# Last layer of a two-layer diffusion trunk: residual and experts' sums on rows of tokens instead of columns

## Chip, cores, metric

One core of one Trainium2 chip. The metric is the device time of one execution in microseconds; lower is better.

## What is computed

A trunk of two layers over 512 latent and 256 context tokens of 1024 channels, batch 1. Each layer adds a token mixer (convolution and RWKV-7 scans) and a hierarchical mixture of 32 experts to the residual, each with a gate per channel (g1, g2). In the last layer only the latent tokens go on. A last RMSNorm with a weight per channel closes the trunk. What the change touches:

```python
# last layer, h2 = modulated norm of x
y2 = hier_moe(h2)            # each token: top group, top 2 experts of 32
                             # sum over both of  gate[token, j] * w2(silu(w1 h2) * (w3 h2))
x = x + g2 * y2              # g2: one number per channel
return x * rsqrt(mean(x*x, axis=-1) + 1e-6) * final_g
```

All data are fp32.

## The kernel before

The residual `xm` is held by columns: channels on the 128 partitions (8 groups, KT = 8), tokens along the free dimension; the latent tokens are its columns from 256 on (`NC_`). In the last layer the 256 columns before them are free.

`moe` (L1154) runs the last stage of a layer. `route` makes, on DVE, for each expert a list of up to 64 tokens (`slot`), the place of its results in the DRAM buffer `bufY` (`dst`), and the gate of each token (`gates`). Then come 32 times `block`: POOL gathers the expert's 64 rows of tokens from DRAM (`xe`), PE turns them to columns, DVE adds the shift (`xs`), PE multiplies with w1 and w3 (streamed, 1 MB a piece, six pieces an expert), ACT and DVE add the halves (`hs`), PE turns again, ACT and DVE make `hid`, PE multiplies with w2 into `py`, ACT and DVE add its halves into `yo` (L1438, L1439), 64 rows of 1024 channels, and POOL scatters these rows into `bufY` (L1440). `route_rest` is called after the first `block` and makes what only the end needs: `rows`, the places in `bufY` of each token's two results, and the sums for the gates. The pieces of w1, w2 and w3 go through three rings of buffers (`er` 5, `ez` 9, `ex` 3); SP issues a load when PE has freed the buffer, in a fixed rotation, so at most 17 pieces lie ahead. `overflow` is a loop over experts with more than 64 tokens; in the profiled execution its body runs no time in the last layer, but all engines pass through its start and its end.

`combine` follows. For each of four tiles of 128 tokens POOL gathers the two rows of every token (`cy`, eight gathers of 512 KB). DVE makes two diagonal matrices from the tokens' gates (`dg`, L1486), PE multiplies with them, which weights the rows, adds the two and turns them to columns (L1493), and DVE adds the result times g2 to `xm` (L1496, 8 per tile). ACT squares (L1499), PE sums the squares over channels with a column of ones (L1501), DVE makes the inverse root for a pair of tiles (`rs_cols`, L295 to L303), PE spreads it over the partitions (`spread`, L309), and DVE writes `xm * final_g * r` (L1510, 8 per pair of tiles). SP stores the pair: two transfers of 1 MB.

The order of the instructions on an engine is fixed when the program is built. Outside of regions marked as ordered by hand a planner picks, with estimated times, the instruction that comes first in the program among those that are ready; it is not bound to the program's order. The `overflow` loop is a border that no instruction crosses. In `route` DVE, ACT and POOL are ordered by hand among themselves.

[...] SBUF buffers named `hs` are two, shared with another tag.

Of the kernel before, what the change touches and what calls it, by code (L numbers as in the profile page):

```python
# [9 lines left out]
F32 = mybir.dt.float32  # L10
# [3 lines left out]
AF = mybir.ActivationFunctionType  # L14
ALU = mybir.AluOpType
# [3 lines left out]
P = 128  # L19
D = 1024  # L20
KT = 8
NC_ = 256
NL = 512
T = NC_ + NL
# [22 lines left out]
CAP = 64  # L47
# [68 lines left out]
class Trunk:  # L116
# [1037 lines left out]
    def moe(self):  # L1154
        nc, tc, t, l, k = self.nc, self.tc, self.t, self.l, self.k
        self.route()
        self.pp.release()
        self.pp = tc.alloc_tile_pool(name=f"pM{l}", bufs=1, space=PSUM)
        self.bp = tc.alloc_tile_pool(name=f"bp{l}", bufs=1, side=self.B, reuse_waits="tile")
        self.gathered = []  # L1160
        with tc.manual_schedule(engines={mybir.EngineType.Pool}):
            for e in range(2):
                self.gathered.append(self.gather(self.slot[:, e:e + 1], True))
        self.prefetch(RING[l][2])
        for e in range(NE):
            self.block(self.slot[:, e:e + 1], lambda: self.dst[:, e:e + 1],
                       t["w1"][l, e], t["w3"][l, e], t["w2"][l, e])
            if e == 0:
                self.route_rest()
        n = 1 if self.full else 0  # L1170
        for i in range(n):
            e = nc.values_load(self.ovt[0:1, i:i + 1], engines=[mybir.EngineType.SP], min_val=0, max_val=NE - 1)
            self.block(self.slot_over[:, i:i + 1], lambda: self.dst[:, NE + i:NE + i + 1], *self.chosen(e))
        self.overflow(n)
        self.bp.release()
        self.ep2.release()
        self.ep.release()
        self.combine()
        self.pp.release()
        self.mp.release()  # L1180

    def route(self):
        e = mybir.EngineType
        with self.tc.manual_schedule(engines={e.DVE, e.Activation, e.Pool}):
            self.route_ordered()
        self.rp.release()
# [213 lines left out]
    def block(self, slot, dst, w1, w3, w2):  # L1400

        nc, k = self.nc, self.k
        xe = self.gathered.pop(0) if self.gathered else self.gather(slot)
        ps = self.psum("px", [P, KT, CAP], 2)
        for kt in range(KT):
            nc.tensor.transpose(ps[:, kt, :], xe[:, kt * P:(kt + 1) * P], k["ident"][:CAP, :CAP])  # L1408
        xs = self.sb(self.wp, [P, 512], "xs", bufs=3, tag="wr")[:].rearrange("p (k t) -> p k t", k=KT)
        nc.vector.tensor_tensor(xs, ps, self.mod[:, 24:32, 0:1].to_broadcast([P, KT, CAP]), op=ALU.add)  # L1410

        def mm(out, a, src, nk, n):
            step = 2048 // n
            for g in range(0, nk, step):
                w = self.ahead.pop(0) if self.ahead else self.expert_weights(src, g, n)
                for i in range(0, step, 2):
                    for c in range(0, n, 512):
                        for h in range(2):
                            kt = g + i + h
                            nc.tensor.matmul(out[h * CAP:(h + 1) * CAP, c:c + 512], a[:, kt, :],  # L1420
                                             w[:, i + h, c:c + 512], start=kt < 2, stop=kt >= nk - 2)

        pt = self.psum("pt", [P, 2, 4, CAP])
        for i, w in enumerate((w1, w3)):
            ps = self.psum("pd", bufs=3)
            mm(ps, xs, w, KT, 512)
            hs = self.hs()[:CAP, :]
            nc.scalar.activation(hs, ps[CAP:], AF.Copy)  # L1428
            nc.vector.tensor_tensor(hs, ps[:CAP], hs, op=ALU.add)  # L1429
            for c in range(4):  # L1430
                nc.tensor.transpose(pt[:, i, c, :], hs[:, c * P:(c + 1) * P], k["ident"][:CAP, :CAP])
        hid = self.sb(self.bp, [P, 4, CAP], "hid", bufs=2)
        nc.scalar.activation(hid, pt[:, 0], AF.Silu)  # L1433
        nc.vector.tensor_tensor(hid, hid, pt[:, 1], op=ALU.mult)  # L1434
        py = self.psum("py", [P, D])
        mm(py, hid, w2, 4, D)
        yo = self.sb(self.bp, [P, D], "yo", bufs=3)[:CAP, :]
        nc.scalar.activation(yo, py[CAP:], AF.Copy)  # L1438
        nc.vector.tensor_tensor(yo, py[:CAP], yo, op=ALU.add)  # L1439
        nc.gpsimd.indirect_dma_start(out=self.bufY[:], out_offset=bass.IndirectOffsetOnAxis(ap=dst(), axis=0), in_=yo,  # L1440
                                     in_offset=None, bounds_check=(NE + NOV) * CAP - 1, oob_is_err=False)

# [4 lines left out]
    def overflow(self, n0):  # L1447
# [3 lines left out]
        with tc.For_i(n0, n, 1) as i:  # L1451
# [4 lines left out]
            nc.sync.dma_start(dst, self.dst[:, bass.ds(NE + i, 1)])  # L1456
            self.block(slot[:], lambda: dst[:], *self.chosen(e))

    def combine(self):

        nc, tc, t, l, k = self.nc, self.tc, self.t, self.l, self.k
        V = nc.vector
        x, lo = self.xm, self.t0
        if not self.last:
            self.normed(self.B)
            self.x_dram = self.dram.tile([P, KT, T], F32, name="x1")
        with tc.tile_pool(name="co", bufs=1, side=self.B, reuse_waits="tile") as cp:
            fg = self.sb(cp, [P, KT], "fg")
            nc.sync.dma_start(fg, t["fg"])
            W = 2 * P  # L1470
            for i0 in (2, 4, 0)[:self.nt // 2] if self.full else (0, 2):
                tok = slice(lo + i0 * P, lo + i0 * P + W)
                s = self.seg(i0)
                sq = self.sb(cp, [P, KT, W], "sq")
# [1 line left out]
                for i in (i0, i0 + 1):  # L1476
                    y = []
                    for j in range(2):
                        g = self.sb(cp, [P, D], f"cy{j}", bufs=4)
                        nc.gpsimd.indirect_dma_start(  # L1480
                            out=g[:], out_offset=None, in_=self.bufY[:],
                            in_offset=bass.IndirectOffsetOnAxis(ap=self.rows[:, i, j:j + 1], axis=0))
# [5 lines left out]
                    for g in range(2):  # L1488
                        ps = self.psum("pd", [P, 4, P], bufs=3)
                        for c in range(4):  # L1490
                            q = slice((4 * g + c) * P, (4 * g + c + 1) * P)
                            for j in range(2):
                                nc.tensor.matmul(ps[:, c, :], y[j][:, q], dg[:, j, :], start=j == 0, stop=j == 1)  # L1493
                        for c in range(4):
                            q = 4 * g + c
# [4 lines left out]
                    for q in range(KT):  # L1500
                        nc.tensor.matmul(pn[:, i - i0:i - i0 + 1], sq[:, q, u], k["ones"][:, :1],  # L1501
                                         start=q == 0, stop=q == KT - 1)
                r = self.rs_cols(cp, pn, 2, 1.0 / D, 1e-6, "c")
                ps = self.psum("px", [P, W], 2)
                for i in range(2):
                    self.spread(ps[:, i * P:(i + 1) * P], r[:, i])
                o = self.sb(cp, [P, KT, W], "fo", bufs=2)
                if self.last:
                    for q in range(KT):
                        V.scalar_tensor_tensor(o[:, q, :], x[:, q, tok], fg[:, q:q + 1], ps, op0=ALU.mult, op1=ALU.mult)  # L1510
                    nc.sync.dma_start(t["out"][:, :, i0 * P:i0 * P + W], o)
                    continue
                nc.sync.dma_start(self.x_dram[:, :, tok], x[:, :, tok])
                n = self.L[l + 1]
                for q in range(KT):
                    b = n["mod"][:, q, s:s + 1]
# [3 lines left out]
                                           op0=ALU.add, op1=ALU.subtract)  # L1520
# [59 lines left out]
```

## Time and profile before

| | us |
|---|---|
| median of three runs | 2935.67 (2931.19 to 2941.17) |
| profiled execution | 2936.51 |
| its span, first to last instruction | 2934.7 |
| experts of the last layer, first transposes to last sum | 2368.7 to 2886.65 |
| first gather of `combine` to the end | 2891.4 to 2934.7 |

Over the span PE is busy 83%, DVE 44%, ACT 29%, POOL 14%; the DMA engines move 251 GB/s on average. These shares are means over stages of different kinds and say little about the last 570 us, in which the change lies. [...]

### The profile page before, as it was taken

To read this page: it belongs to the slowest core of one execution; us is meant where nothing else is said; L and a number is where in the kernel's file an instruction comes from. 1 tells how busy PE (TensorE), PEld (TensorE's weight loads), DVE (VectorE), ACT (ScalarE), POOL (GpSimd) and SP (SyncE) were. 2 spreads that over 40 slices of the span, in tenths; PEclk is the share of its full clock that TensorE was granted. 3 is DMA by queue.
4 is the path that set the end of the run, shared out by engine and by line. 5 is a ranking of instruction groups with operands and counts; after the bars stand their busy time and mean duration, and the time that the engine had idled before them with its cause. 6 is when DMAs were issued, how large, how long until landed. Compare 5 with 4: busy or idle time off the path is not lost. (4 is left out here: it accounts for less than half of the span.)

```text
span 2934.7 us, 43704 instructions
## 1 busy us (share of the span) xinstructions
PE 2445.0 (83%) x17177; PEld 1557.8 (53%) x17177; DVE 1304.1 (44%) x2757; ACT 852.2 (29%) x1637; POOL 403.5 (14%) x509
## 2 busy tenths in 40 slices
PE   6898899998889496778877998788988769697886
PEld 4676677777778232223326775566766633232334
DVE  4576654636463321112225685566546422122223
ACT  4444333333223121111112553343432401111111
POOL 0122011111100101101102231011210011111101
PEclk9899998999999698888997998789989879897898
DMA  7657554553563999999965367454445599999983
GB/s 292 211 153 226 168 169 159 185 172 111 173 216 112 329 403 401 385 397 395 404 256 180 112 192 241 162 171 163 152 130 183 213 350 403 404 401 404 405 354 113
DMA packets 287136, 737.13 MB, mean 251 GB/s; under 512 B 57168, under 2 KB 144464, under 8 KB 230864
## 3 DMA queue, kind: packets, MB, share of 16 engines
q1 hardware_dynamic: 272208, 697.59, 65.7%
q0 software_dynamic: 13280, 31.48, 3.3%
q10 hardware_dynamic: 1440, 5.24, 0.4%
q8 instruction: 136, 2.23, 0.3%
q14 instruction: 72, 0.59, 0.1%
HBM read 647.44 MB, written 99.88 MB: 255 GB/s over the span
## 5 line engine op out<-in xcount | busy, mean ns | idle before, releaser
L332 PE MATMUL pd<-hh,wh 128*128 128x512 f32 (+1 forms) x912 | 354.2, 428 | 16.5 <-ACT wh L313 7.9
L332 PE MATMUL pd<-hh,wl 128*128 128x512 f32 (+1 forms) x912 | 312.5, 383 | 10.1 <-DVE wl L314 10.1
L332 PE MATMUL pd<-hl,wh 128*128 128x512 f32 (+1 forms) x912 | 311.6, 382 | 1.1 <-DVE hl L314 1.1
L1420 PE MATMUL pd<-ez,xs 128*64 128x512 f32 x1072 | 266.7, 608 | 12.4 <-DMA ez<-in_w 12.4
L314 DVE TENSOR_TENSOR wl<-wr,wh 128x512 fp32r<-128x512 f32 x236 | 166.5, 706 | 241.3 <-ACT wh L313 240.7
L1420 PE MATMUL pd<-er,xs 128*64 128x512 f32 x640 | 183.2, 669 | 75.4 <-DMA er<-in_w 75.4
L1428 ACT ACTIVATE hs<-pd 64x512 f32<-64x512 f32 x130 | 75.4, 592 | 574.0 <-PE pd L1420 500.8
L313 ACT ACTIVATE wh<-wr 128x512 fp32r<-128x512 f32 x236 | 148.5, 630 | 286.5 <-PE pd L332 169.3
L1429 DVE TENSOR_TENSOR hs<-pd,hs 64x512 f32<-64x512 f32 x130 | 87.2, 680 | 300.7 <-ACT hs L1428 300.7
L332 PEld LDWEIGHTS pd<-hh,wh 128*128 128x128 f32 x912 | 163.9, 198 | 100.0 <-issue 34.6
L332 PEld LDWEIGHTS pd<-hh,wl 128*128 128x128 f32 x912 | 163.9, 198 | 46.2 <-DVE wl L314 13.5
L332 PEld LDWEIGHTS pd<-hl,wh 128*128 128x128 f32 x912 | 165.3, 199 | 29.4 <-DVE hl L314 2.1
L1420 PE MATMUL py<-ez,hid 128*64 128x512 f32 x560 | 154.1, 688 | 24.9 <-DVE yo L1439 24.9
L1420 PEld LDWEIGHTS pd<-ez,xs 128*64 128x64 f32 x1072 | 83.1, 141 | 155.7 <-issue 129.3
L1410 DVE TENSOR_TENSOR xs<-px,mod 128x512 f32<-128x512 f32 x65 | 44.9, 690 | 240.3 <-PE pd L1420 153.8
L1395 POOL DMA_INDIRECT xe<-h2rows,slot x64 | 61.1, 954 | 624.1 <-PE px L1408 569.5
L1420 PEld LDWEIGHTS pd<-er,xs 128*64 128x64 f32 x640 | 51.5, 152 | 174.1 <-issue 90.5
L1434 DVE TENSOR_TENSOR hid<-hid,pt 128x256 f32<-128x256 f32 x65 | 27.0, 415 | 215.4 <-ACT hid L1433 215.4
L1420 PE MATMUL pd<-ex,xs 128*64 128x512 f32 x368 | 103.5, 654 | 22.1 <-DMA ex<-in_w 22.1
L1439 DVE TENSOR_TENSOR yo<-py,yo 64x1024 f32<-64x1024 f32 x65 | 78.9, 1214 | 94.4 <-ACT yo L1438 82.6
L1440 POOL DMA_INDIRECT bufY<-yo,dst x65 | 59.7, 918 | 349.3 <-DVE yo L1439 218.5
L1420 PEld LDWEIGHTS py<-ez,hid 128*64 128x64 f32 x560 | 47.6, 158 | 112.7 <-issue 104.0
(379 smaller groups left out, 4447.0 us busy)
## 6 DMA issues: line engine op xcount, KB each, us to landing
ez<-in_w SPq DMA_DIRECT2D x204, 1024.0 KB, 16.2
er<-in_w SPq DMA_DIRECT2D x120, 1024.0 KB, 16.4
ex<-in_w SPq DMA_DIRECT2D x66, 1024.0 KB, 17.3
wm<-in_w_mod SPq DMA_DIRECT2D x48, 1024.0 KB, 6.6
wr<-in_w_in SPq DMA_DIRECT2D x172, 256.0 KB, 3.2
bufY<-zrow SPq DMA_DIRECT2D x28, 512.0 KB, 6.7
dKB<-KB SPq DMA_DIRECT2D x16, 768.0 KB, 5.1
dRR<-RR SPq DMA_DIRECT2D x16, 768.0 KB, 4.7
```

What stands on the lines that cost most here:

```text
L313: self.nc.scalar.activation(hi, src, AF.Copy)
L314: self.nc.vector.tensor_tensor(lo, src, hi, op=ALU.subtract)
L332: nc.tensor.matmul(p, a[:, k], h[:, kt, s], start=kt == 0 and j == 0, stop=kt == nk - 1 and j == 2)
L1395: self.nc.gpsimd.indirect_dma_start(out=xe[:], out_offset=None, in_=self.h2[:], in_offset=bass.IndirectOffsetOnAxis(ap=slot, axis=0), boun ...
L1410: nc.vector.tensor_tensor(xs, ps, self.mod[:, 24:32, 0:1].to_broadcast([P, KT, CAP]), op=ALU.add)
L1420: nc.tensor.matmul(out[h * CAP:(h + 1) * CAP, c:c + 512], a[:, kt, :], w[:, i + h, c:c + 512], start=kt < 2, stop=kt >= nk - 2)
L1428: nc.scalar.activation(hs, ps[CAP:], AF.Copy)
L1429: nc.vector.tensor_tensor(hs, ps[:CAP], hs, op=ALU.add)
L1434: nc.vector.tensor_tensor(hid, hid, pt[:, 1], op=ALU.mult)
L1439: nc.vector.tensor_tensor(yo, py[:CAP], yo, op=ALU.add)
L1440: nc.gpsimd.indirect_dma_start(out=self.bufY[:], out_offset=bass.IndirectOffsetOnAxis(ap=dst(), axis=0), in_=yo, in_offset=None, bounds_ch ...
```

## The change

In the last layer alone:

- `row_consts`, before the first expert: loads final_g and makes g2 and final_g into rows that stand on all partitions (`grow`, `frow`), kept in the free columns of `xm`. Each takes 8 DVE products with the identity, 8 PE products with a matrix of ones, 2 ACT copies.
- `turn(kt)`, before experts 1 to 8: PE turns the four 128x128 squares of one channel group of `xm` to rows of tokens, ACT copies them back in place.
- In each `block`: `yo` is multiplied by `grow` on DVE ahead of the scatter (also in the body of `overflow`).
- `combine_rows` instead of `combine`: eight gathers into eight buffers of their own; for each tile two scalar_tensor_tensor on 128x1024 (a row times the token's gate, plus the residual; the other row times its gate, plus that); a square with a sum along the row on ACT; the inverse root per pair; one scalar_tensor_tensor (times r, times `frow`); a store of 512 KB per tile. PE is not used.
- The output tensor has rows of tokens instead of columns.

Layer 0 keeps `combine`; its branches for the last layer are cut out.

```diff
--- before.py
+++ after.py
@@ -1162,7 +1162,11 @@
             for e in range(2):
                 self.gathered.append(self.gather(self.slot[:, e:e + 1], True))
         self.prefetch(RING[l][2])
+        if self.last:
+            self.row_consts()
         for e in range(NE):
+            if self.last and 1 <= e <= KT:
+                self.turn(e - 1)
             self.block(self.slot[:, e:e + 1], lambda: self.dst[:, e:e + 1],
                        t["w1"][l, e], t["w3"][l, e], t["w2"][l, e])
             if e == 0:
@@ -1175,9 +1179,41 @@
         self.bp.release()
         self.ep2.release()
         self.ep.release()
-        self.combine()
+        if self.last:
+            self.combine_rows()
+        else:
+            self.combine()
         self.pp.release()
         self.mp.release()
+
+    def row_of(self, n, col):
+
+
+        nc, k = self.nc, self.k
+        row = self.xm[:, 4 * n:4 * n + 4, :NC_]
+        for g in range(2):
+            ds = self.hs()[:].rearrange("p (a b) -> p a b", a=4)
+            ps = self.psum("pd", [P, 4, P], 3)
+            for c in range(4):
+                nc.vector.tensor_scalar(ds[:, c, :], k["ident"], col[:, 4 * g + c:4 * g + c + 1], None, op0=ALU.mult)
+                nc.tensor.matmul(ps[:, c, :], k["ones"], ds[:, c, :], start=True, stop=True)
+            nc.scalar.activation(row[:, 2 * g:2 * g + 2], ps[:].rearrange("p (a c) b -> p a (c b)", a=2), AF.Copy)
+        return row
+
+    def row_consts(self):
+
+        fg = self.sb(self.mp, [P, KT], "fg")
+        self.nc.sync.dma_start(fg, self.t["fg"])
+        self.grow = self.row_of(0, self.mod[:, 40:48, 0])
+        self.frow = self.row_of(1, fg)
+
+    def turn(self, kt):
+
+        nc = self.nc
+        ps = self.psum("pd", [P, 4, P], 3)
+        for i in range(4):
+            nc.tensor.transpose(ps[:, i, :], self.xm[:, kt, NC_ + i * P:NC_ + i * P + P], self.k["ident"])
+        nc.scalar.activation(self.xm[:, kt, NC_:], ps[:].rearrange("p a b -> p (a b)"), AF.Copy)
 
     def route(self):
         e = mybir.EngineType
@@ -1437,6 +1473,9 @@
         yo = self.sb(self.bp, [P, D], "yo", bufs=3)[:CAP, :]
         nc.scalar.activation(yo, py[CAP:], AF.Copy)
         nc.vector.tensor_tensor(yo, py[:CAP], yo, op=ALU.add)
+        if self.last:
+            yg = yo.rearrange("p (a b) -> p a b", a=4)
+            nc.vector.tensor_tensor(yg, yg, self.grow[:CAP], op=ALU.mult)
         nc.gpsimd.indirect_dma_start(out=self.bufY[:], out_offset=bass.IndirectOffsetOnAxis(ap=dst(), axis=0), in_=yo,
                                      in_offset=None, bounds_check=(NE + NOV) * CAP - 1, oob_is_err=False)
 
@@ -1456,19 +1495,45 @@
             nc.sync.dma_start(dst, self.dst[:, bass.ds(NE + i, 1)])
             self.block(slot[:], lambda: dst[:], *self.chosen(e))
 
+    def combine_rows(self):
+
+        nc, tc, t = self.nc, self.tc, self.t
+        V = nc.vector
+        with tc.tile_pool(name="co", bufs=1, side=self.B, reuse_waits="tile") as cp:
+            ys = []
+            for i in range(4):
+                for j in range(2):
+                    y = self.sb(cp, [P, D], f"cy{i}{j}")
+                    nc.gpsimd.indirect_dma_start(
+                        out=y[:], out_offset=None, in_=self.bufY[:],
+                        in_offset=bass.IndirectOffsetOnAxis(ap=self.rows[:, i, j:j + 1], axis=0))
+                    ys.append(y)
+            for i0 in (0, 2):
+                ss = self.sb(cp, [P, 2], "ss", bufs=2)
+                for i in (i0, i0 + 1):
+                    a, b = ys[2 * i], ys[2 * i + 1]
+                    av = a[:].rearrange("p (k c) -> p k c", k=KT)
+                    V.scalar_tensor_tensor(av, av, self.gates[:, i, 0:1], self.xm[:, :, NC_ + i * P:NC_ + i * P + P],
+                                           op0=ALU.mult, op1=ALU.add)
+                    V.scalar_tensor_tensor(b, b, self.gates[:, i, 1:2], a, op0=ALU.mult, op1=ALU.add)
+                    nc.scalar.activation(a, b, AF.Square, accum_out=ss[:, i - i0:i - i0 + 1])
+                r = self.rs_cols(cp, ss, 2, 1.0 / D, 1e-6, f"c{i0}")
+                for i in (i0, i0 + 1):
+                    b = ys[2 * i + 1]
+                    bv = b[:].rearrange("p (a c) -> p a c", a=4)
+                    V.scalar_tensor_tensor(bv, bv, r[:, i - i0], self.frow, op0=ALU.mult, op1=ALU.mult)
+                    nc.sync.dma_start(t["out"][i * P:(i + 1) * P, :], b)
+
     def combine(self):
 
         nc, tc, t, l, k = self.nc, self.tc, self.t, self.l, self.k
         V = nc.vector
         x, lo = self.xm, self.t0
-        if not self.last:
-            self.normed(self.B)
-            self.x_dram = self.dram.tile([P, KT, T], F32, name="x1")
+        self.normed(self.B)
+        self.x_dram = self.dram.tile([P, KT, T], F32, name="x1")
         with tc.tile_pool(name="co", bufs=1, side=self.B, reuse_waits="tile") as cp:
-            fg = self.sb(cp, [P, KT], "fg")
-            nc.sync.dma_start(fg, t["fg"])
             W = 2 * P
-            for i0 in (2, 4, 0)[:self.nt // 2] if self.full else (0, 2):
+            for i0 in (2, 4, 0):
                 tok = slice(lo + i0 * P, lo + i0 * P + W)
                 s = self.seg(i0)
                 sq = self.sb(cp, [P, KT, W], "sq")
@@ -1505,11 +1570,6 @@
                 for i in range(2):
                     self.spread(ps[:, i * P:(i + 1) * P], r[:, i])
                 o = self.sb(cp, [P, KT, W], "fo", bufs=2)
-                if self.last:
-                    for q in range(KT):
-                        V.scalar_tensor_tensor(o[:, q, :], x[:, q, tok], fg[:, q:q + 1], ps, op0=ALU.mult, op1=ALU.mult)
-                    nc.sync.dma_start(t["out"][:, :, i0 * P:i0 * P + W], o)
-                    continue
                 nc.sync.dma_start(self.x_dram[:, :, tok], x[:, :, tok])
                 n = self.L[l + 1]
                 for q in range(KT):
@@ -1571,9 +1631,9 @@
     nc = bacc.Bacc("TRN2", target_bir_lowering=False, num_devices=1)
     t = {n: nc.dram_tensor("in_" + n, a.shape, mybir.dt.from_np(a.dtype), kind="ExternalInput").ap()
          for n, a in arrays.items()}
-    t["out"] = nc.dram_tensor("out", (P, KT, NL), F32, kind="ExternalOutput").ap()
+    t["out"] = nc.dram_tensor("out", (NL, D), F32, kind="ExternalOutput").ap()
     with tile.TileContext(nc, schedule_with_timeline_sim=True) as tc:
         Trunk(tc, t).build()
     r = run_bass_kernel_spmd(nc, [{"in_" + n: a for n, a in arrays.items()}], core_ids=[0])
     y = r.results[0]["out"]
-    return np.ascontiguousarray(y.transpose(2, 1, 0)).reshape(1, NL, D)
+    return np.ascontiguousarray(y).reshape(1, NL, D)
```

## Rows read from the trace of the kernel before

**Rows 1.** Stretches: columns PE, PEld, DVE, ACT, POOL busy, clock, DMA share, GB/s.

```profile
2352.00:2368.70 16.70, 0.00 (x0) 0.01 (x1) 0.18 (x1) 0.00 (x0) 3.92 (x4) 0.50 1.01 415
2372.70:2376.40 3.70, 3.70 (x11) 1.23 (x12) 0.69 (x1) 0.00 (x0) 0.94 (x1) 0.50 0.12 35
2410.00:2828.00 418.00, 348.37 (x1680) 128.48 (x1678) 93.45 (x132) 64.77 (x105) 45.77 (x49) 0.89 1.01 406
2834.30:2870.60 36.30, 36.28 (x163) 12.20 (x163) 7.91 (x10) 6.86 (x11) 2.69 (x3) 0.95 0.60 222
2904.00:2906.00 2.00, 2.00 (x20) 2.00 (x20) 1.73 (x8) 1.04 (x1) 0.00 (x0) 1.00 0.79 324
```

**Rows 2.** Timeline, PE: start us, us, instruction [idle before, releaser].

```profile
2834.32 3.68 PE L1420 MATMUL pd<-er,xs 128*64 128x512 f32 x8 [5.76 <-DMA er<-in_w]
```

**Rows 3.** Timeline, DVE and PE, the last two experts.

```profile
2877.40 1.22 DVE L1439 TENSOR_TENSOR yo<-py,yo 64x1024 f32<-64x1024 f32 x1 [4.21 <-ACT yo L1438]
2878.54 0.40 DVE L1434 TENSOR_TENSOR hid<-hid,pt 128x256 f32<-128x256 f32 x1
...
2879.00 5.32 PE L1420 MATMUL py<-er,hid 128*64 128x512 f32 x16 [2.31 <-DVE hid L1434]
...
2885.43 1.22 DVE L1439 TENSOR_TENSOR yo<-py,yo 64x1024 f32<-64x1024 f32 x1 [6.48 <-ACTq L1451]
```

**Rows 4.** Chain of waits, two links: start us, us, what.

```profile
2898.14 10.31 PE pd L1493 x70
...
2926.71 2.35 DVE fo L1510 x6
```

**Rows 5.** Timeline, POOL: first and last of the eight gathers.

```profile
2891.43 0.98 POOL L1480 DMA_INDIRECT cy<-bufY,rows  x1 [3.62 <-DVE dg L1486]
...
2900.20 0.94 POOL L1480 DMA_INDIRECT cy<-bufY,rows  x1 [0.31 <-issue]
```

**Rows 6.** Groups by form: busy us, mean ns | idle before, releasers.

```profile
L1206 DVE SCALAR_TENSOR_TENSOR hr<-hr,mr,srow 128x1024 f32<-128x1024 f32 x2 | 2.5, 1275 | 0.0
...
L1499 ACT ACTIVATE sq<-xm 128x1024 f32<-128x1024 f32 x4 | 4.2, 1057 | 30.7 <-DVE xm L1496 24.4 <-DVE cz L299 6.2
```

**Rows 7.** Timeline, DVE: first and last instruction of an inverse root.

```profile
2922.34 0.16 DVE L295 TENSOR_SCALAR cv<-px 128x2 f32<-128x2 f32 x1
...
2924.30 0.16 DVE L303 SCALAR_TENSOR_TENSOR cr<-cz,cg 128x2 f32<-128x2 f32 x1
```

**Rows 8.** DMA issues: count, KB each, median us to landing.

```profile
out<-fo SPq DMA_DIRECT2D x2, 1024.0 KB, 4.5
...
bufY<-yo,dst POOLq DMA_INDIRECT x1, 2.7
...
ex<-in_w SPq DMA_DIRECT2D x3, 1024.0 KB, 8.2
```

**Rows 9.** Timeline, all engines: from the ring loads to the first freed buffer.

```profile
2360.17 1.28 SPq L1141 DMA_DIRECT2D ex<-in_w  x3
...
2368.72 1.08 PE L1408 MATMUL px<-cst,xe 64*128 64x64 f32 x8 [17.18 <-DMA xe<-h2rows,slot]
...
2376.42 0.33 SPq L1141 DMA_DIRECT2D er<-in_w  x1
```

**Rows 10.** One line's instructions: ns min/median/max, first and last start.

```profile
L309 PE MATMUL px<-cst,cr x8: 275/363/551, 2917.9 to 2925.4; 128*128 128x128 f32 x8
...
L1198 PE MATMUL pA<-cst,xa x32: 272/272/327, 2287.5 to 2335.5; 128*128 128x128 f32 x32
```

**Rows 11.** Timeline, DVE: a sum of route_rest.

```profile
2343.73 0.17 DVE L1371 TENSOR_REDUCE pg<-ge 128x4 f32<-128x16 f32 x1
```

**Rows 12.** Timeline of layer 0's gathers, and all twenty by line.

```profile
1549.54 0.69 DVE L314 TENSOR_TENSOR wl<-wr,wh 128x512 fp32r<-128x512 f32 x1 [0.27 <-ACT wh L313]
...
1549.71 1.33 POOL L1480 DMA_INDIRECT cy<-bufY,rows  x1 [0.30 <-issue]
...
L1480 POOL DMA_INDIRECT cy<-bufY,rows x20: 933/938/1330, 1545.9 to 2900.2; - x20
```

## Prediction, made before the change was run

> **What bounds the kernel now.** I read four views, from coarse to fine: stretches by engine, the chain of waits, the order of instructions around its links, and groups by form for durations. The change touches only the experts of the last layer (from 2352 us on) and what follows them, so the 2350 us before are left alone.
>
> In the stretches [rows 1] the reader is to see three regimes. From 2410 to 2828 us the DMA share is 1.01 and PE is busy 348 of 418 us: the stream of expert weights sets the pace, and extra PE, ACT or DVE work hides as long as PE keeps freeing buffers. The last time PE waits for a weight block is before 2834.32, for 5.76 us [rows 2]; from there to 2870.6 PE is busy 36.28 of 36.30 us while DMA falls to 0.60. So the last two to three experts are bound by PE and by what PE waits for. Third, the tail: the chain of waits [rows 4] runs from the second gather's landing at 2898.14 through 70 PE records (10.31 us) and on to the last normalisation on DVE, which ends at 2926.71 + 2.35 = 2929.06. The end lies 5.6 us later, at 2934.7: the output transfer (4.5 us from issue to landing [rows 8]) and about 1 us.
>
> A fourth place matters though it is short: the start of the experts. From 2352 to 2368.7 PE, ACT and DVE have next to nothing to do while DMA is full; from 2372.7 to 2376.4 DMA is at 0.12, because all rings are full and nothing is freed [rows 1]. The stream restarts at 2376.42 [rows 9], when the first expert's products have freed a buffer. After that it is saturated, so whatever delays the first block delays the end one for one.
>
> **The tail, rebuilt on rows of tokens.** Removed from the path: the gated sums on PE, the updates of xm on DVE (8 per tile), the column sums of squares, the spread of r and the normalisations by column (8 per pair). From the second gather's landing (2898.14) to the last of them (2929.06) these take 30.9 us.
>
> Put in: per tile of 128 tokens two gated sums and one scaling, each a scalar_tensor_tensor on 128x1024, all in SBUF. The very form stands in the trace: L1206, 1.275 us [rows 6]. That is 12 instructions. The first needs only the first gather and runs while the second lands; 11 x 1.275 = 14.0 us remain. The two inverse roots stay: one takes 2924.30 + 0.16 - 2922.34 = 2.1 us for 11 instructions [rows 7], two 4.2 us. Gaps between DVE instructions and short waits for the later gathers: 0.5 us, an estimate. The gathers themselves are no bound: the last is issued at 2900.20 [rows 5] and DMA is done with them before 2906 [rows 1], when DVE still has more than 11 us to do.
>
> Between a pair's sums and its inverse root stands a square on ACT: 1.06 us without the sum [rows 6]; with accum_out no row exists, and with its two hand-overs I estimate 1.4 us. If the pairs run strictly one after the other, DVE waits 1.4 us twice, 2.8 us. If the order fills these waits with the other pair's instructions, 0. I take 0.7, near the filled end, because the order is one by readiness: a sum of the routing that stands after the first expert in the program (L1371) ran at 2343.73 [rows 11], 25 us ahead of that expert's first transposes [rows 9].
>
> So 14.0 + 4.2 + 0.5 + 0.7 = 19.4 us instead of 30.9: -11.5 us, with ends -12.2 (no wait) and -9.4 (both).
>
> The output now leaves as four transfers of 512 KB, the last alone behind the last scaling. 1024 KB take 4.5 us to land, 256 KB of expert rows 2.7 [rows 8]; between them some 3.3 us: -1.2, with ends 0 and -1.8.
>
> The first gather now starts just behind a DVE instruction of the removed code [rows 5]. Without it, 0 to -0.6; I take -0.3.
>
> **The gate at each expert's rows.** 32 more tensor_tensor on 64x1024 on DVE; the nearest form is L1439, 1.22 us [rows 3]. In the weight-bound stretch DVE is busy 93 of 418 us, so the 1.22 us per expert hide there; queued behind such a multiplication are the next block's hs, xs and hid on DVE, and PE waits for these. The cover is the weight stream; without it they would cost up to 32 x 1.22 = 39 us. It is gone for the last experts. There I go through the DVE order: behind the last expert's sum (2885.43) the multiplication stands before the scatter on POOL, +1.22 with certainty. Behind the sum before it (2877.40 + 1.22 = 2878.62) comes hid at 2878.54, and PE waits 2.31 us for this hid at 2879.00 [rows 3]. The multiplication is ready at the same moment and earlier in the program, so I put it first: +1.22, with 0 as the other end. The earlier ones fall into idle time of DVE (7.91 of 36.3 us busy from 2834.3 on [rows 1]).
>
> **The start of the experts.** Two constant rows need 16 DVE instructions, 16 PE products and 4 ACT copies; eight turns need 32 PE transposes and 8 ACT copies of 128x512. A product like these (L309, two records each) has records of 275 to 551 ns, so about 0.3 us per product at the high clock and 0.6 at the low one; a transpose (L1198) takes 0.27 us, at the low clock an estimated 0.54 [rows 10]. Nothing in them depends on an expert, so by the order by readiness they go into the gap before the first expert's transposes (2368.72 [rows 9]), 16.7 us in which PE does nothing [rows 1]. At the high clock they need 16 x 0.3 + 32 x 0.27 = 13.4 us, at the low clock 16 x 0.6 + 32 x 0.54 = 26.9 us. [...] So the gap takes most of the work, and either a bit sticks out or the clock is up when the first block begins (its first products, 3.7 us of low clock, would then take half). I take 0, with -2.5 and +4 as ends. Also moved: the load of final_g, 4 KB, from behind the experts to SP's queue beside the three ring loads; behind it on SP only weight loads are queued, and on DVE the second constant row waits for it.
>
> **The sum.** -11.5 - 1.2 - 0.3 + 1.2 + 1.2 + 0 = -10.6 us. The profiled execution took 2936.51 us (span 2934.7 and 1.8 around it), 0.84 above the median of the runs; so 2925.9 for an execution like it, 2925.1 against the median. Ends of the terms together: -16 to -3 us, 2920 to 2933.
>
> **The rivals.** *Gathers and DVE hinder each other, and pairs run in order.* DVE now works on two SBUF inputs while POOL still issues gathers. One row of layer 0 speaks for it: the gather at 1549.71 takes 1.33 us, while a DVE instruction with two SBUF inputs runs from 1549.54 [rows 12], against 0.94 for the one of [rows 5]. Six gathers, 2 to 7, lie after DVE's start; up to 1.2 us of wait for four of them makes the last land near 2911, and DVE itself could be held 4 x 0.94 us. With +3.8 us for that and +2.1 for strict order of the pairs the gain shrinks to 4.7 us: 2931, no change that can be measured. I give it 0.29; the median of all twenty gathers is 938 ns and this is the longest [rows 12].
>
> [...]
>
> *The first block comes late (slower).* PE's order is fixed beforehand, by estimated times. If all of the added PE work stands ahead of the first expert's transposes and the clock stays low, 26.9 us go into a gap of 16.7: 10 us late. If final_g is also queued behind the three ring loads, issued by 2361.45 [rows 9] and 8.2 us later in SBUF [rows 8], the second constant row begins near 2369.7, and 4.8 us of its products and 17 us of transposes follow: first transposes at 2391.5, 23 us late. The stream restarts late by as much. The sign turns at 10.6 us late; at 23 us the time is 2925.1 + 23 = 2948. Against it: the order by readiness of [rows 11], by which a load that waits for nothing goes ahead of ring loads that wait for memory (no row of a load shows it). I give 0.11 to a delay beyond 19 us.
>
> *The change does less than it says:* the gate's multiplications delay hid and hs of the last three experts each time (3 x 1.22 more) - this lies within the first rival's time, and I count it there.
>
> **How the numbers follow.** Forecast 2925 us: 0.60. First rival, 2931: 0.29. Late start, 2948: 0.11. About 0.3%, 8.8 us, is what a measurement of this kernel can tell from no change: faster by more 0.60, within 0.29, slower by more 0.11. The range takes the forecast's ends and the first rival with a late start of up to 6 us, and leaves out the longer delays: 2919 to 2937.
>
> **What would show it.** Right: from the second gather's landing to the last scaling some 19 to 20 us; DVE nearly closed there; L1206's duration in the new sums; the scatter of the last expert 1.2 us behind its sum; PE's added work before 2369 and the weight stream's restart near 2376. Wrong: a restart after 2380; gathers longer than 0.94 us beside DVE sums and holes of 1 us or more in DVE between them; a last output transfer that lands later than 4 us after its issue; PE waiting for DVE before 2828 often enough that the weight stream drops below a share of 1.0.

## The result

The changed kernel takes 2915.35 us (median of 8 runs, 2903.7 to 2922.97) where the kernel before, run beside it, takes 2932.23 (median of 8, 2923.62 to 2941.17). The ratio is 0.9935 [0.992, 0.9949]: faster by 0.65%, some 17 to 19 us, and below the low end of the predicted range. The two profiled executions have spans of 2934.7 and 2913.5 us, 21.2 us apart. I cut both at three points that stand in both traces: the first ring buffer that is freed in the last layer (the first `er` load behind the `ex` loads), the last expert's sum on DVE, and the first gather of the combination. For before these lines stand in [rows 9], [rows 3] and [rows 5]; the first point of after is this line of its SP timeline, and the other two stand in the view of its tail below.

```profile
2376.76 2.04 SPq L1141 DMA_DIRECT2D er<-in_w  x2
```

| | before, us | after, us | difference | forecast |
|---|---|---|---|---|
| start to first freed buffer | 2376.42 | 2376.76 | +0.3 | 0 |
| to the start of the last expert's sum | 509.0 | 500.2 | -8.8 | +1.2 |
| to the first gather | 6.00 | 7.26 | +1.3 | +0.9 |
| to the end | 43.3 | 29.3 | -14.0 | -12.7 |
| sum | 2934.7 | 2913.5 | -21.2 | -10.6 |

The forecast time, 2925.1, was counted from a median of 2935.67 for the kernel before; beside the change it took 2932.23, so 3.4 of the 9.8 us between forecast and measured time lie in the reference.

(The tail's -12.7 is -11.5 - 1.2; the +0.9 is +1.2 - 0.3.) Three of the four steps lie near their forecast. The second, 500 us in which the weights of 32 experts stream in, was to be left alone and gave 8.8 us. Most of the experiments are about it.

**The tail.** The timeline of after, DVE and POOL, from the last expert's sum to the last store (start us, us, instruction [idle before, releaser]):

```profile
2876.92 1.22 DVE L1475 TENSOR_TENSOR yo<-py,yo 64x1024 f32<-64x1024 f32 x1 [5.37 <-ACTq L1490]
2878.17 1.22 DVE L1478 TENSOR_TENSOR yo<-yo,xm 64x1024 f32<-64x1024 f32 x1
2879.66 0.90 POOL L1479 DMA_INDIRECT bufY<-yo,dst  x1 [6.94 <-DVEq L1490]
2884.18 0.97 POOL L1507 DMA_INDIRECT cy<-bufY,rows  x1 [3.62 <-issue]
...
2888.54 1.29 DVE L1516 SCALAR_TENSOR_TENSOR cy<-cy,gates,xm 128x1024 f32<-128x1024 f32 x1 [9.15 <-DMA cy<-bufY,rows]
2889.21 1.42 POOL L1507 DMA_INDIRECT cy<-bufY,rows  x1 [0.31 <-issue]
2890.88 1.32 DVE L1518 SCALAR_TENSOR_TENSOR cy<-cy,gates,cy 128x1024 f32<-128x1024 f32 x1 [1.05 <-DMA cy<-bufY,rows]
2890.94 0.94 POOL L1507 DMA_INDIRECT cy<-bufY,rows  x1 [0.30 <-issue]
2892.12 1.32 DVE L1516 SCALAR_TENSOR_TENSOR cy<-cy,gates,xm 128x1024 f32<-128x1024 f32 x1
2892.18 0.94 POOL L1507 DMA_INDIRECT cy<-bufY,rows  x1 [0.30 <-issue]
...
2894.30 1.28 DVE L1518 SCALAR_TENSOR_TENSOR cy<-cy,gates,cy 128x1024 f32<-128x1024 f32 x1 [0.86 <-DMA cy<-bufY,rows]
...
2895.84 1.28 DVE L1516 SCALAR_TENSOR_TENSOR cy<-cy,gates,xm 128x1024 f32<-128x1024 f32 x1 [0.26 <-DMA cy<-bufY,rows]
...
2897.04 0.16 DVE L295 TENSOR_SCALAR c0v<-ss 128x2 f32<-128x2 f32 x1
...
2897.31 1.28 DVE L1518 SCALAR_TENSOR_TENSOR cy<-cy,gates,cy 128x1024 f32<-128x1024 f32 x1
...
2902.53 0.17 DVE L295 TENSOR_SCALAR c2v<-ss 128x2 f32<-128x2 f32 x1 [0.16 <-ACT cy L1519]
...
2903.91 5.88 SPq L1525 DMA_DIRECT2D out<-cy  x4
...
2906.96 2.48 DVE L1524 SCALAR_TENSOR_TENSOR cy<-cy,c2r,xm 128x1024 f32<-128x1024 f32 x2
```

From the second gather's landing (2890.88) to the end of the last scaling (2906.96 + 2.48 = 2909.44) are 18.6 us, where [rows 4] had 30.9. The end comes 4.1 us later instead of 5.6. DVE is nearly closed: it waits 0.86 and 0.26 us for gathers and 0.16 us for one square. The first pair's inverse root (L295 at 2897.04) runs between the sums of the second pair, so the order is one by readiness. The last expert's sum is followed by the gate's multiplication (L1478) and only then by the scatter: that is the 1.25 us more before the first gather.

**The weight stream.** The stretch of before from 2420 to 2820 us (columns as in [rows 1]; the clock is the share of TensorE's full speed that was granted):

```profile
2420.00:2820.00 400.00, 331.75 (x1613) 122.99 (x1610) 89.90 (x128) 62.99 (x103) 44.87 (x48) 0.90 1.01 405
```

The same stretch of after:

```profile
2420.00:2820.00 400.00, 337.05 (x1644) 125.39 (x1638) 120.92 (x155) 65.57 (x107) 45.12 (x48) 0.91 1.01 412
```

The DMA share is 1.01 in both, so the stream is the bound in both, but it moves 412 GB/s instead of 405, 1.7% more. Over some 500 us that is 8 us, what the second line of the table gained. Engines issue more work than before (DVE 121 us busy instead of 90), the weights are the same bytes, and yet they come faster. Layer 0, which loads its weights by the same lines, has 395 GB/s in both traces between 1010 and 1490 us.

### The profile page after: what moved, and what is told of

Read it like the earlier page. It is cut to its first block, busy times and chain, and to the rows that moved or that the text cites. A ratio compares the mean times of both kernels' runs of the same rounds, so it can differ in the third digit from the quotient of the medians.

```text
span 2913.5 us, 43460 instructions
## 1 busy us (share of the span) xinstructions
PE 2428.9 (83%) x17041; PEld 1539.9 (53%) x17041; DVE 1345.1 (46%) x2761; ACT 859.3 (29%) x1653; POOL 402.9 (14%) x509
## 5 line engine op out<-in xcount | busy, mean ns | idle before, releaser
L332 PE MATMUL pd<-hh,wl 128*128 128x512 f32 (+1 forms) x912 | 310.5, 381 | 10.6 <-DVE wl L314 10.6
```

Source lines behind the costliest of these rows:

```text
L332: nc.tensor.matmul(p, a[:, k], h[:, kt, s], start=kt == 0 and j == 0, stop=kt == nk - 1 and j == 2)
```

## Experiments

All ratios are to the kernel before, run on the same chip; "stretch" is the time from the first freed ring buffer to the start of the last expert's sum, "tail" from the first gather to the end, both of the profiled execution.

**1 and 2. Is the gain in the stretch there again?** The kernel before and the kernel after, unchanged, once more.

> The kernel before, unchanged, profiled once more. In the first pair of traces the weight stream of the last layer moved 405 GB/s before and 412 GB/s after the change (2420 to 2820 us), and the last expert's sum came 8.5 us earlier after it, which the prediction does not have. Theory A (the stream's rate differs from one execution to the next, whatever the kernel): from the first freed ring buffer to the last expert's sum this trace shows something else than 509 us, by 3 us or more either way, and the time ratio to the kernel before is 1.000 within its interval. Theory B (the change speeds the stream): this trace repeats 509 us within 2 us.

> The changed kernel, unchanged, profiled once more. From the first freed ring buffer to the last expert's sum the first trace showed 500 us. Theory A (rate differs between executions): 500 to 510 us, no closer to 500 than to the kernel before's 509. Theory B (the change speeds the stream): 500 us within 2. Under both: from the second gather's landing to the last scaling 18.5 us, from the first gather's issue to the end 29.3 us, ratio 0.993 to 0.996 (A: -13 us, 0.9956; B: -21 us, 0.993).

Before again: 0.999 [0.9973, 1.0007], stretch 509.0, tail 43.4, 404 GB/s. After again: 0.9943 [0.9921, 0.9966], stretch 502.4, tail 28.8, 412 GB/s. So both gains repeat. The first 2380 us scatter more than the steps to be explained: the first freed buffer comes at 2373.49 in the one and at 2380.66 in the other, with the same instructions ahead of it except the two constant rows. The stretches are therefore compared from that point on.

**3. The gate alone.** The constant row of g2 and the 32 multiplications, with the columns kept in the tail, whose update takes 1.0 in place of g2.

```diff
+        if self.last:
+            self.grow = self.row_of(0, self.mod[:, 40:48, 0])
...
+        if self.last:
+            yg = yo.rearrange("p (a b) -> p a b", a=4)
+            nc.vector.tensor_tensor(yg, yg, self.grow[:CAP], op=ALU.mult)
```

> Only the gate's part: the kernel before, with g2 made into a row ahead of the experts and multiplied into the experts' rows on DVE; the sums, the norm and the output stay on columns, with g2 left out of them. Theory A: the last layer's experts last as long as before within what executions differ, the scatter of the last expert comes 1.2 us later, the time is 0 to +2 us (ratio 1.000 to 1.001). Theory B in the form that the 32 multiplications on DVE change the pace of the experts for the better: 6 to 8 us less from the first freed buffer to the last sum, ratio 0.9975 to 0.998.

1.0006 [0.9989, 1.0023]; stretch 509.0, last sum to first gather 7.26, tail 42.7. The 32 multiplications are covered by the stream, as priced, and add their 1.26 us only at the end. They do not make the stream faster. The timeline of this kernel's POOL also settles the wait for `dg`:

```profile
2884.59 0.90 POOL L1459 DMA_INDIRECT bufY<-yo,dst  x1 [6.85 <-DVEq L1470]
2889.11 0.97 POOL L1499 DMA_INDIRECT cy<-bufY,rows  x1 [3.62 <-DVE dg L1505]
```

Scatter to gather is 4.52 us here and 4.52 in after (2879.66 to 2884.18), where no `dg` exists any more and the same 3.62 us of idle time stand as "issue". The wait named in [rows 5] cost nothing.

**4. The turns, twice.** The kernel before, which turns the residual to rows ahead of experts 1 to 8 and back ahead of experts 9 to 16.

```diff
+            if self.last and 1 <= e <= 2 * KT:
+                self.turn((e - 1) % KT)
```

> Only the turns: the kernel before, with the residual turned to rows ahead of experts 1 to 8 and turned back ahead of experts 9 to 16, so that the sums and the norm on columns stay as they were. 64 PE transposes and 16 ACT copies more. Theory A: hidden, ratio 1.000 within 0.001; the late-start rival of the prediction would show as a first freed buffer later than 2377 us. Theory B in the form that the turns shift the order of PE and ring frees for the better: 6 to 8 us less in the experts, ratio 0.9975 to 0.998.

1.0004 [0.9988, 1.002]; stretch 505.4, 405 GB/s between 2420 and 2820 us. Twice the turns (64 PE transposes and 16 copies on ACT instead of 32 and 8) can't be seen in the time. The stretch is 3.6 us shorter here, at the old rate of the stream; the turns add work and take none away, so I don't put that down to them. The first freed buffer comes at 2366.13, so no late start shows either. The 412 GB/s come neither from the gate alone nor from the turns alone.

**5. Other addresses, same instructions.** What is left is both together, with the order planned around them, and where the buffers lie. `fg`, 32 bytes on each partition, was allocated after the rings were released in the kernel before, and is allocated ahead of them now; the `er` and `ez` buffers of the last layer (14 of the 17) start 32 bytes lower: at addresses that leave 32 when divided by 512 in the kernel before (161312 for the first `er`), at multiples of 512 in the kernel after (161280). A tile of the kernel before is made 32 bytes longer, and nothing else is touched.

```diff
-        self.ovt = self.sb(mp, [P, NOV + 1], "ovt", I32)
+        self.ovt = self.sb(mp, [P, NOV + 1 + 8 * self.last], "ovt", I32)
```

> The kernel before with one small tile of the last layer's pool made 32 bytes longer per partition: no instruction and no order differs, only the addresses of the buffers that lie behind that pool, 14 of the 17 ring buffers of the last layer's expert weights, move by 32 bytes, to where the changed kernel has them (its tile for final_g, 32 bytes, lies in the same pool). They then begin at multiples of 512 bytes; in the kernel before they begin 32 bytes behind one. Theory C (the stream is faster because of where its buffers begin): from the first freed buffer to the last sum 500 to 503 us instead of 509, some 412 GB/s instead of 405, ratio 0.997 to 0.998. Theory D (gate, turns and the order planned around them do it together): 509 us, ratio 1.000.

0.9977 [0.9965, 0.999]; stretch 502.1 us, tail 43.4. The row of the stretch:

```profile
2420.00:2820.00 400.00, 332.14 (x1634) 123.61 (x1630) 91.73 (x129) 63.79 (x103) 45.74 (x49) 0.91 1.01 411
```

The two ends of the stretch, from this kernel's timelines of SP and DVE:

```profile
2376.71 2.51 SPq L1141 DMA_DIRECT2D er<-in_w  x2
...
2878.83 1.22 DVE L1439 TENSOR_TENSOR yo<-py,yo 64x1024 f32<-64x1024 f32 x1 [6.50 <-ACTq L1451]
```

The kernel before gains 6.9 us in the stretch, and 6 GB/s, from addresses alone.

**6 and 7. The kernel after, moved off.** The same tile of the kernel after longer by 32 bytes and by 64, so that the 14 buffers leave 480 and 448 when divided by 512.

> The changed kernel with the same small tile 32 bytes longer: no instruction and no order differs, the 14 ring buffers move 32 bytes further and begin 32 bytes off a multiple of 64. Theory C: 508 to 510 us from the first freed buffer to the last sum instead of 500 to 502, 405 GB/s, and the ratio to the kernel before becomes what the tail alone is worth: -13 us, 0.9955 to 0.9965. Theory D: 500 to 502 us, ratio as the changed kernel's, 0.994.

> The changed kernel with that tile 64 bytes longer: the 14 ring buffers begin at a multiple of 64 bytes, but not of 128, 256 or 512. Theory C with 64 bytes as the step: as the changed kernel, 500 to 503 us. Theory C with a longer step: 508 to 510 us, as with 32 bytes. Theory D: 500 to 503 us.

By 32: 0.9952 [0.9935, 0.997], stretch 508.9, tail 29.7. By 64: 0.9973 [0.996, 0.9985], stretch 509.1, tail 29.1, 406 GB/s. The row for 32:

```profile
2420.00:2820.00 400.00, 332.71 (x1636) 123.61 (x1634) 117.26 (x150) 65.44 (x106) 44.25 (x47) 0.91 1.01 406
```

And the two ends of its stretch:

```profile
2381.86 2.78 SPq L1141 DMA_DIRECT2D er<-in_w  x2
...
2890.80 1.22 DVE L1475 TENSOR_TENSOR yo<-py,yo 64x1024 f32<-64x1024 f32 x1 [5.37 <-ACTq L1490]
```

The tail keeps its gain and the stretch has lost all of its own: back at 509 us with all the new work in it. So the change has two parts, and each can be had without the other: experiment 5 has the one, experiments 6 and 7 have the other.

**8. The gate in the tail.** The change without its multiplications in the experts; g2 is applied to the gathered rows instead.

```diff
-                    V.scalar_tensor_tensor(av, av, self.gates[:, i, 0:1], self.xm[...], op0=ALU.mult, op1=ALU.add)
-                    V.scalar_tensor_tensor(b, b, self.gates[:, i, 1:2], a, op0=ALU.mult, op1=ALU.add)
+                    V.scalar_tensor_tensor(ag, ag, self.gates[:, i, 0:1], self.grow, op0=ALU.mult, op1=ALU.mult)
+                    V.tensor_tensor(av, av, self.xm[...], op=ALU.add)
+                    V.scalar_tensor_tensor(bg, bg, self.gates[:, i, 1:2], self.grow, op0=ALU.mult, op1=ALU.mult)
+                    V.tensor_tensor(b, b, a, op=ALU.add)
```

> The changed kernel with the gate taken out of the experts and applied in the tail: two more DVE instructions on 128x1024 per tile, 8 x 1.22 = 9.8 us, in the stretch that DVE bounds; the scatter of the last expert comes 1.2 us earlier. If the 32 multiplications beside the experts are covered by the weight stream, as the prediction has it: from the first freed buffer to the last sum the same 500 to 503 us as the changed kernel, tail 29.3 + 9.8 = 39 us, +8.6 us in all against the changed kernel, ratio about 0.997. If they cost time beside the experts: the experts shorter by more than 2 us.

0.9978 [0.9965, 0.9991]; stretch 505.6, last sum to first gather 6.01, tail 35.7, 410 GB/s. Neither the stretch (500 to 503 expected) nor the tail (39 expected) came as expected; the stretch is taken up behind experiment 11. Against after the tail is 6.4 us longer and the way to the first gather 1.25 shorter. The eight added instructions take 8 x 1.22 = 9.8 us, from the groups of DVE in this kernel's tail:

```profile
L1515 DVE TENSOR_TENSOR cy<-cy,xm 128x1024 f32<-128x1024 f32 x4 | 4.9, 1220 | 0.0
L1518 DVE TENSOR_TENSOR cy<-cy,cy 128x1024 f32<-128x1024 f32 x4 | 4.9, 1220 | 0.0
```

3.4 us less than that show in the time. About 2.2 of it are waits that the added work fills: behind its first sum after's DVE waits 1.05, 0.86 and 0.26 us for gathers and 0.16 for a square, this kernel's only 0.17 for a square. Another 0.6 is that the records of neighbouring instructions overlap: from its own start to the next one's, the eight take 1.13 to 1.19 us, 9.15 in all. The rest is not traced further. In the experts the gate costs 1.25 us and in the tail 6.4, so the place the change chose is right.

**9. Both layers on multiples of 512.** The kernel after, with layer 0's ring buffers moved too: two tiles of layer 0 get 224 and 160 bytes more.

```diff
-        self.ovt = self.sb(mp, [P, NOV + 1], "ovt", I32)
+        self.ovt = self.sb(mp, [P, NOV + 1 + (0 if self.last else 56)], "ovt", I32)
...
-        yo = self.sb(self.bp, [P, D], "yo", bufs=3)[:CAP, :]
+        yo = self.sb(self.bp, [P, D + (0 if self.last else 40)], "yo", bufs=3)[:CAP, :D]
```

> The changed kernel with two tiles of layer 0 made longer (224 and 3 x 160 bytes per partition): no instruction and no order differs, but all 17 ring buffers of layer 0's expert weights now begin at multiples of 512 bytes instead of 288 and 480 bytes behind one; the last layer's addresses stay. If it is the buffers' place that sets the stream's rate, layer 0's experts, so far at 395 GB/s between 1010 and 1490 us, run at 405 to 412 GB/s and last 10 to 18 us less; ratio to the kernel before 0.988 to 0.991, faster than both. If the last layer's gain came from something else: 395 GB/s, ratio 0.994.

2905.94 us (2898.43 to 2908.19), ratio 0.9905 [0.9887, 0.9923]: the fastest kernel of the study, and below both. The stretch in layer 0, of after:

```profile
1010.00:1490.00 480.00, 386.65 (x1872) 142.99 (x1872) 107.30 (x164) 69.99 (x113) 50.38 (x54) 0.89 1.01 395
```

And of this kernel:

```profile
1010.00:1490.00 480.00, 390.20 (x1897) 143.99 (x1894) 107.08 (x159) 72.45 (x117) 50.41 (x54) 0.91 1.01 401
```

From layer 0's first freed buffer to its last sum are 542.4 us in after and 533.9 here, 8.5 less; in the other twelve profiles this stretch takes 538.4 to 544.4 us, mean 541.7. The last layer's stretch is 501.6. So the same cause in another place gives about the same 8 us. It is less than the 10 to 18 us expected, and the rate stays under the 405 to 412 GB/s expected: what keeps layer 0 at 401 where the last layer has 412 stays open.

**10 and 11. Which multiple.** The kernel after with its 14 buffers at addresses that leave 256, and 128, when divided by 512 (the tile longer by 256 and by 384 bytes).

> The changed kernel with the last layer's 14 ring buffers moved by 256 bytes: they begin 256 bytes behind a multiple of 512. If 512 is the step: 508 to 510 us from the first freed buffer to the last sum, 405 GB/s. If 128 or 256 is enough: 500 to 503 us, 412 GB/s.

> The same with 384 bytes: the buffers begin 128 bytes behind a multiple of 512. If 256 or 512 is the step: 508 to 510 us; if 128 is enough: 500 to 503 us. The two together tell the step; 64 bytes were not enough (509.1 us).

At 256: 0.9937 [0.992, 0.9954], stretch 500.8, tail 28.9. At 128: 0.9962 [0.995, 0.9975], stretch 507.6, tail 30.1. The DMA view of the first from 2420 to 2820 us (throughput in 40 slices of 10 us, then packets and the mean):

```profile
GB/s 424 425 406 397 429 394 406 430 400 406 421 417 409 401 412 404 388 412 415 393 424 408 403 427 428 413 413 422 376 425 423 384 408 416 415 411 428 421 428 426
DMA packets 25608, 164.90 MB, mean 412 GB/s; under 512 B 4735, under 2 KB 4735, under 8 KB 6254
```

And of the second:

```profile
GB/s 422 418 401 407 410 421 390 389 405 413 398 404 404 423 358 411 394 391 406 408 388 421 404 403 421 422 404 416 405 369 422 422 392 401 417 417 406 416 415 419
DMA packets 25220, 162.54 MB, mean 406 GB/s; under 512 B 4648, under 2 KB 4648, under 8 KB 6140
```

The best slices show it most plainly: up to 430 GB/s at 256, at most 423 at 128. The packets have the same mix of sizes in both (18.5 and 18.4% of them under 512 B) and the DMA engines are equally full (the loads' queue has 96.4% of their time in both), so a packet takes a little longer at 128. The packet records of the traces agree: from 2420 to 2820 us the median packet of 8 KB takes 309 ns in each of the six profiles with the 14 buffers at multiples of 256, and 312 or 313 in each of the seven others; in layer 0, from 1010 to 1490 us, 309 in experiment 9 and 313 in all others.

Taken together, by what the addresses of the 14 buffers leave when divided by 256: at 0 (after, its repeat and experiments 5, 8, 9, 10) the rate between 2420 and 2820 us is 410 to 413 GB/s, at 32, 128, 192 and 224 (before, its repeat and experiments 3, 4, 6, 7, 11) it is 400 to 406. The stretches are 500.2 to 502.4 us against 507.6 to 509.1, with two that lie between: experiment 4 with 505.4 and experiment 8, whose buffers are at 0, with 505.6. By their rates (405 and 410 GB/s) and their packets (313 and 309 ns) each belongs to its group. What moved them lies at the ends of the stretch. Experiment 8 moves 341 GB/s in its first 43.67 us, where after moves 363 in 43.24, and from PE's last wait for a ring load to the last sum it takes 54.39 us where after takes 51.76. In experiment 4 PE's last two waits for ring loads are 0.98 and 0.47 us long, where before waits 5.76 [rows 2]. The program of each has an order of its own; what in that order does it is not traced further. The experiments ran on three chips (1 to 4, 5 to 8, 9 to 11), and both groups stand on each of them.

## Why the prediction was wrong where it was, and right where it was

**The step that failed** is the weight stream of the last layer, which has no term in the sum: between the first block and the last experts the prediction expected added work to hide under it and nothing else to change. It read the change as a list of instructions. The diff also moves an allocation: `fg` goes from the pool of the tail to the pool of the whole stage, ahead of the rings. I costed its load (4 KB, one DMA) and not its 32 bytes. The prediction took the weight stream's rate as given ("the stream of expert weights sets the pace") and named as a sign of error there only a share below 1.0; the share stayed at 1.01, the rate went from 405 to 412 GB/s, and the stretch took 8.8 us less where +1.2 was forecast. Shown by experiments 5 to 7, 9, 10 and 11: the stretch follows the addresses, whichever kernel's instructions run in it.

The sizes, from the first freed buffer to the end: 558.3 and 558.4 us in the two profiles of before; 545.9, 545.4 and 544.9 in after at the three remainders that are no multiple of 256, mean 545.4; 536.7, 538.4 and 537.0 in after at multiples of 256, mean 537.4 (538.0 in experiment 9). So what I set out to price is worth 558.35 - 545.4 = 12.9 us, and the addresses give 8.0 more (6.9 in the order of the kernel before, experiment 5). Against the 10.6 forecast the first is 2.3 off; without the addresses the time would have lain inside the range, as that of experiments 6 and 7 does (2920.72 and 2925.64).

**The tail**, forecast at -11.5 and -1.2, measured -14.0 in one pair and -13.2 to -14.6 over all kernels with the new tail in its own form. The working held: the sums and scalings take 1.28 to 1.32 us each (L1206's 1.275 of [rows 6]). Three of its small terms were off. The wait for squares is 0.16 us, not 0.7, because pairs interleave; waits for gathers are 0.86 + 0.26 us where all gaps together had 0.5. And 18.6 - 11 x 1.28 - 1.3 of waits leaves 3.2 us for the two inverse roots, where [rows 7] gave 4.2: records overlap, so lengths added up say too much (L295 from 2902.53 for 0.17, the next scaling from 2902.61; a sum from 2890.88 for 1.32, the next from 2892.12). The second inverse root, taken alone, still spans the 2.1 us of [rows 7], the scalings within it left out. The chain of waits of after shows that the gathers are closer to the bound than I said:

```profile
2889.21 6.60 DMA cy<-bufY,rows
2895.84 1.28 DVE cy L1516
...
2901.35 1.06 ACT cy L1519
2902.41 0.10 ACTq L1635
2902.53 0.17 DVE c2v L295
...
2908.24 1.20 DVEq L1635
```

It runs from one gather's landing (6.60 us) through the second pair's sums, one square and the second inverse root. PE, which had 10.31 us in [rows 4], is gone.

**The gate at the rows.** +1.2 behind the last sum was right (1.25). The +1.2 behind the sum before it was not incurred: I put the multiplication ahead of `hid`, and DVE's order has `hid` first, so PE waits the same 2.31 us as in [rows 3]. This is after's timeline there:

```profile
2870.01 0.40 DVE L1470 TENSOR_TENSOR hid<-hid,pt 128x256 f32<-128x256 f32 x1
2870.34 1.21 DVE L1478 TENSOR_TENSOR yo<-yo,xm 64x1024 f32<-64x1024 f32 x1
2870.47 5.35 PE L1456 MATMUL py<-er,hid 128*64 128x512 f32 x16 [2.31 <-DVE hid L1470]
```

The first gather's -0.3 did not come (experiment 3).

**The start.** The late first block did not happen: the stream restarts 0.3 us later than before. (Counted from the three `ex` loads, the first buffer comes free 16.3 and 16.5 us later in the two profiles of before, and 16.5 to 17.6 in those with the new tail.) One reason I gave for that was wrong in part. The constant rows do go into the gap, 32 records of PE from 2351.06 on:

```profile
2351.06 6.02 PE L1199 MATMUL pd<-hs,cst 128*128 128x128 f32 x32 [0.37 <-DVE slot L1333]
```

They take 6.0 us at a mean granted clock of 0.61, between my 4.8 and 9.6; at the first block, from 2372 to 2376 us, the clock is 0.50 in both kernels. The turns are not in the gap at all: the first runs at 2393.4, in the experts' stream, which covers them (experiment 4). So nothing of the 17 us of transposes could stand in front of the first block.

**The rival on gathers and DVE.** It shows in part: in after the gather at 2889.21, begun 0.67 us into a DVE sum on two SBUF inputs, takes 1.42 us. Those at 2890.94 and 2892.18, which begin 0.06 us behind such a sum's start, take 0.94. Other profiles of the same instructions show more of it: the last four gathers take 1.45, 1.93, 1.61 and 1.19 us in experiment 11 and 1.54, 1.81, 1.25 and 1.38 in experiment 6, all begun while such a sum runs. That is 2.4 and 2.2 us over four of 0.94, and these two have the longest tails, 30.1 and 29.7 us against 28.8 to 29.3. So the price differs between executions of one order, and 1.3 us lie between the longest and the shortest of these tails. No run shows the 3.8 us for which the rival has DVE held: after's eight sums take 1.28 to 1.32 us, beside gathers and without. The rival's other half, strict order of the pairs, did not occur. What decides whether a gather beside such a sum takes longer is not shown.

## What to carry to other kernels

When a diff adds, drops or moves a buffer, look where the buffers behind it come to lie, as one looks at the instructions: in a stretch that is bound by DMA, 32 bytes gave 8.0 us where the whole rework of the tail with its gate gave 12.9. Compare the rate of the stream in GB/s, not only its share of busy time, which stayed at 1.01 here while the rate moved. And try the targets of a weight stream on multiples of 256 bytes first, since it costs a few bytes, and price other changes from there.

## What the runs showed of the hardware that was not expected

In a stretch that is nearly all loads of 1024 KB into SBUF, 8 KB to each partition, the DMA engines moved 410 to 413 GB/s when 14 of 17 target buffers began at a multiple of 256 bytes, and 404 to 406 when they began 32, 128, 192 or 224 bytes past one (400 in experiment 3, whose stretch is as long as that of before). The median packet of 8 KB took 309 ns in the first case and 312 or 313 in the second; in layer 0, with all 17 at multiples of 256, 401 instead of 393 to 396. Whether the cause is the write into SBUF itself or something ahead of it, and whether addresses between those tried behave like either, these runs don't tell: only whole sets of buffers were moved, together with the smaller tiles that lie behind the same pad.
